# Norm statistics per token: sums of squares as 128x2 numbers, spread by a diagonal product

## The chip, the cores and the metric

The kernel runs on one core of a Trainium2 chip. The metric is device time in microseconds (us) of one execution, the median of several runs. Less is better.

## What is computed

Two layers of a hybrid decoder trunk for 256 tokens of width 2048, float32. Each layer has a mixer (layer 0: dilated attention beside a gated linear recurrence; layer 1: window attention beside a state-space layer) and a ConvFFN, and each of these four parts reads a normed and modulated copy of x. A fifth norm ends the kernel.

```python
def rmsnorm(x, g):
    y = x32 * lax.rsqrt(jnp.mean(x32 * x32, axis=-1, keepdims=True) + NORM_EPS)
    return (y * g.astype(F32)).astype(x.dtype)

def modulate(h, shift, scale):
    return h * (1.0 + scale[:, None]) + shift[:, None]

for layer in range(DEPTH):                      # 2 layers
    h = modulate(rmsnorm(x, norm_mix[layer]), sh1, sc1)
    x = x + g1 * mixer(h)
    h = modulate(rmsnorm(x, norm_ffn[layer]), sh2, sc2)
    x = x + g2 * conv_ffn(h)
return rmsnorm(x, norm_final)
```

shift, scale and gate come from a conditioning vector by the "ada" weights, 1 MB for each column of 128 outputs.

## The kernel before

x lies on the chip transposed: 16 tiles `x[i]`, each with 128 channels on the partitions and the 256 tokens along the free axis. All weights (some 590 MB) are streamed once through six buffers of 1 MB ("w", WB = 6), issued by the SP queue. A weight tile is split by ScalarE (`hi`, L379 or L330) and VectorE (`lo`, L380 or L331) into two float32r parts, and a product is made of three passes (hi by x_hi, hi by x_lo, lo by x_hi). The ada weights go through the same six buffers. Each of their 192 tiles is multiplied with the conditioning and summed by one VectorE instruction of 128x2048 (L221).

A planner (the tile framework) orders each engine's queue before the run, by priorities and by its own estimate of times; an engine works its queue in that order.

`rms` (L258) makes the factor r = 1/sqrt(mean + eps) for all 256 tokens, the same row on all partitions:

- ScalarE squares the 16 tiles (L264).
- In the four later norms VectorE adds the squares (L272), all but the last; then two float32 products with a 128x128 matrix of ones sum over the partitions (each is two passes of 256 columns on TensorE). In the first norm (`on_pe`) TensorE takes all 16 squares, 16 products of two passes.
- ScalarE takes the root of the 128x256 result in PSUM (L280), VectorE its reciprocal, 128x256 (L284).
- In norms two to four `WARM` = (0, 4) puts four more products with ones behind the sum, which only keep TensorE busy (L282).

`modulated_tile` (L287) then makes the tiles that the next weight stage reads: x[i] * A * r on VectorE (L289), + shift on ScalarE (L291, and L293 for the unsplit copy that the first stage uses), the low part on VectorE (L294). The next stage ("slab") goes by k-tiles: seven or fewer PSUM banks take the products of k-tile 0, then of k-tile 1, and so on. So TensorE can't start a slab before k-tile 0 is modulated, and r needs the last piece of x, which needs the last product of the stage before.

PSUM has 8 banks: 3 "mm", 3 "sp", 2 "sx". All matrix products are recorded as L138. The five norms lie at about 11, 408, 1209, 1508 and 2259 us of the profiled span; the last is followed only by the scaling (L996) and the store of the output.

In the first stage (ev_a, up to 84 us) each k-tile needs two ada tiles, which VectorE works at the same time as the small preparations of the state-space layer (L1024 to L1079).

Of the kernel before, what the change touches and what calls it, by code (L numbers as in the profile page):

```python
# [50 lines left out]
WARM = ((0, 0), (0, 4), (0, 4), (0, 4))  # L51
WARM_AT = 13
# [43 lines left out]
def trunk(ctx: ExitStack, tc: tile.TileContext, a: dict, out: bass.AP):  # L96
# [54 lines left out]
    def pin():  # L151
        """the next product comes after all the products before it"""
        pinned[0] = PIN

    def start(chain, prio=0):
        """a chain of work whose parts go between pieces of the weight stream"""
        chains.append((chain, prio))
        advance(chains[-1])
# [15 lines left out]
    # ---------------------------------------------------------------- inputs that are needed first  # L174
# [28 lines left out]
    # silu(c), the same row on all partitions  # L203
# [10 lines left out]
    # ---------------------------------------------------------------- adaLN: one column of 128 at a time  # L214
# [27 lines left out]
    def gate_of(l, q):  # L242
        """gate(i): columns i and i + 1 of a gate"""
# [13 lines left out]
    # ---------------------------------------------------------------- norm  # L257
    def rms(on_pe=False, warm=(0, 0)):  # L258
        """1 / sqrt(mean(x^2) + eps); warm: products that only keep the array's clock up, before the sum and after"""
        ps = pss()  # L260
        acc = None
        for i in range(KT):
# [4 lines left out]
            if on_pe:  # L267
                mm(ps[:, :T], ones, sq, i == 0, i == KT - 1)
            elif acc is None:
                acc = sq  # L270
            elif i < KT - 1:
                V.tensor_tensor(acc, acc, sq, op=ALU.add)  # L272
            if i == WARM_AT:
                for n in range(warm[0]):
                    mm(ps[:, T:], ones, sq, n == 0, n == warm[0] - 1)
        if not on_pe:
            mm(ps[:, :T], ones, acc, True, False)
            mm(ps[:, :T], ones, sq, False, True)
        rt = t1()
        S.activation(rt, ps[:, :T], AF.Sqrt, bias=epsb, scale=1.0 / D)  # L280
        for n in range(warm[1]):
            mm(ps[:, T:], ones, sq, n == 0 and OWN, n == warm[1] - 1)  # L282
        r = t1()
        V.reciprocal(r, rt)  # L284
        return r

    def modulated_tile(i, r, A, sh, full=None):  # L287
        t = t1()
# [9 lines left out]
    def modulator(l, q, g, on_pe=False):  # L298
        """h[i](): the i-th k-tile of the normed and modulated x; q: the chunk of the shift"""
# [21 lines left out]
    # ---------------------------------------------------------------- weight streams  # L321
# [1027 lines left out]
```

## Time and profile before

| | |
|---|---|
| runs | 2271.8, 2273.1, 2273.46 us |
| median | 2273.1 us |
| span of the profiled execution | 2271.8 us |
| TensorE busy | 2209.5 us (97%) |
| VectorE busy | 1812.8 us (80%) |
| ScalarE busy | 1221.4 us (54%) |
| mean granted TensorE clock | 0.988 of full |

In rows of a timeline the first number is the start in us from the span's start, the second the time in us, then engine and line, operation, output <- inputs, shape, and how many instructions the row merges. Matmuls overlap in the array, so of a row with n passes the distance of two starts is (time less one pass's own time) / (n - 1). PEld is TensorE's load of weights, which runs beside its products.

### The profile page before, as it was taken

The page shows a single profiled execution, that of the slowest core. Times are in us where ns is not written, and L with a number is a line of the kernel's source. Part 1 is how long each engine was busy: PE and PEld are TensorE (multiplying, and loading weights), DVE is VectorE, ACT ScalarE, POOL GpSimd, SP SyncE. Part 2 cuts the span into 40 slices and gives each one's busy share as a digit, 9 for nine tenths or more (in the row PEclk, how much of TensorE's full clock was granted, in tenths as well). Part 3 has the DMA queues.
Part 4 walks back from the last instruction along what each step waited for, and adds up shares of the span by engine and source line. Part 5 has one row for each costly group of instructions (what it writes and reads, how often), then busy time and mean ns, then how long its engine had stood idle before and what let it go on. Part 6 is the DMA issues. An engine that isn't in the chain of part 4 may idle for free. (4 is left out here: it accounts for less than half of the span.)

```text
span 2271.8 us, 42923 instructions
## 1 busy us (share of the span) xinstructions
PE 2209.5 (97%) x17498; PEld 2148.6 (95%) x17498; DVE 1812.8 (80%) x2908; ACT 1221.4 (54%) x2056; POOL 4.4 (0%) x12
## 2 busy tenths in 40 slices
PE   7999999998999999999999999999999999999997
PEld 4899989898999999999999899999999999999997
DVE  7789989989998869989778778986888657666655
ACT  3355856444775456654445767644565434544543
POOL 0000000000000000000000000000000000000000
PEclk9999999999999999999999999999999999999998
DMA  9988689888669778888866665967756667655541
GB/s 349 373 337 308 235 303 350 333 327 338 259 242 352 306 295 317 320 336 314 304 238 224 245 254 224 342 222 289 276 181 222 238 244 287 234 185 180 203 181 69
DMA packets 106088, 615.43 MB, mean 271 GB/s; under 512 B 12065, under 2 KB 14625, under 8 KB 54817
## 3 DMA queue, kind: packets, MB, share of 16 engines
q1 hardware_dynamic: 105890, 612.69, 71.9%
q8 instruction: 137, 2.24, 0.4%
q14 instruction: 61, 0.50, 0.1%
HBM read 592.72 MB, written 18.87 MB: 269 GB/s over the span
## 5 line engine op out<-in xcount | busy, mean ns | idle before, releaser
L138 PE MATMUL mm<-t,hi 128*128 128x256 f32 x9568 | 1744.2, 284 | 7.3 <-ACT hi L379 4.3
L138 PEld LDWEIGHTS mm<-t,hi 128*128 128x128 f32 x9568 | 1498.5, 193 | 10.4 <-ACT hi L379 4.7
L138 PE MATMUL mm<-t,lo 128*128 128x256 f32 x4784 | 1356.7, 284 | 5.1 <-DVE lo L331 5.1
L138 PEld LDWEIGHTS mm<-t,lo 128*128 128x128 f32 x4784 | 919.8, 192 | 7.3 <-DVE lo L331 5.8
L330 ACT CAST hi<-w 128x1024 fp32r<-128x1024 f32 (+1 forms) x558 | 565.4, 1016 | 594.4 <-PE mm L138 523.2
L331 DVE TENSOR_TENSOR lo<-w,hi 128x1024 fp32r<-128x1024 f32 (+1 forms) x558 | 657.5, 1182 | 280.2 <-ACT hi L330 276.3
L221 DVE CUSTOM_DVE_ANT_0 ada<-ada,cond 128x2048 f32<-128x2048 f32 x192 | 438.3, 2283 | 22.7 <-DMA ada<-in_adaT 19.7
L379 ACT CAST hi<-w 128x768 fp32r<-128x768 f32 (+2 forms) x160 | 146.4, 921 | 163.1 <-PE sx L138 86.6
L380 DVE TENSOR_TENSOR lo<-w,hi 128x768 fp32r<-128x768 f32 (+2 forms) x160 | 167.4, 1061 | 62.3 <-ACT hi L379 61.6
L138 PE MATMUL sp<-t,hi 128*128 128x256 f32 x832 | 153.6, 283 | 0.0
L138 PEld LDWEIGHTS sp<-t,hi 128*128 128x128 f32 x832 | 130.3, 192 | 0.8 <-ACT hi L379 0.2
L138 PE MATMUL sp<-t,lo 128*128 128x256 f32 x416 | 117.1, 283 | 0.0
L759 DVE SCALAR_TENSOR_TENSOR t<-mm,ffn_p,t 128x255 f32<-128x255 f32 x232 | 110.6, 477 | 4.2 <-ACT t L757 1.7
L138 PEld LDWEIGHTS sp<-t,lo 128*128 128x128 f32 x416 | 79.6, 192 | 0.1
L291 ACT ACTIVATE t<-t,mods 128x256 fp32r<-128x256 f32 x64 | 30.0, 505 | 85.6 <-DVE mods L311 62.8
L138 PE MATMUL sx<-t,t 128*128 128x64 f32 (+2 forms) x480 | 68.3, 283 | 3.3 <-DMA t<-s 1.1
L757 ACT ACTIVATE t<-mm,ffn_p 128x256 f32<-128x256 f32 x116 | 65.0, 560 | 5.6 <-DVE t L759 5.4
L138 PEld LDWEIGHTS sx<-t,t 128*128 128x128 f32 x480 | 61.5, 194 | 5.9 <-issue 3.3
L264 ACT ACTIVATE t<-x 128x256 f32<-128x256 f32 x80 | 31.9, 414 | 59.4 <-DVE x L451 31.9
L138 PE MATMUL mm<-t,w 128*128 128x256 f32 x256 | 56.5, 379 | 0.9 <-ACT t L665 0.9
L138 PEld LDWEIGHTS mm<-t,w 128*128 128x128 f32 x256 | 48.5, 190 | 7.8 <-ACT t L665 1.3
L318 ACT CAST t<-t 128x256 fp32r<-128x256 f32 x102 | 40.2, 402 | 26.1 <-DVE t L763 20.1
(264 smaller groups left out, 1475.1 us busy)
## 6 DMA issues: line engine op xcount, KB each, us to landing
ada<-in_adaT SPq DMA_DIRECT2D x192, 1024.0 KB, 6.5
w<-in_ffn_in SPq DMA_DIRECT2D x116, 1024.0 KB, 6.1
w<-in_ffn_out SPq DMA_DIRECT2D x80, 896.0 KB, 4.7
w<-in_ffn_first SPq DMA_DIRECT2D x48, 896.0 KB, 6.6
w<-in_ev_out SPq DMA_DIRECT2D x16, 1024.0 KB, 6.4
w<-in_ffn_out SPq DMA_DIRECT2D x16, 1024.0 KB, 5.2
w<-in_od_out SPq DMA_DIRECT2D x16, 1024.0 KB, 7.4
w<-in_ev_a SPq DMA_DIRECT2D x16, 896.0 KB, 7.0
```

Of the source, the lines that this page charges most:

```text
L138: keep(PE.matmul(o, l, r, start=start, stop=stop, skip_group_check=True))
L221: V.tensor_tensor_reduce(out=w, in0=w, in1=cond, scale=1.0, scalar=0.0, op0=ALU.mult, op1=ALU.add, accum_out=mods[l][:, j:j + 1])
L264: S.activation(sq, x[i], AF.Square)
L291: S.activation(o[:, 0, :], t, AF.Identity, bias=sh[:, i:i + 1])
L318: S.copy(o[:, 0, :], src)
L330: S.copy(hi[:, :m], w[:, o:o + m])
L331: V.tensor_tensor(lo[:, :m], w[:, o:o + m], hi[:, :m].bitcast(F32), op=ALU.subtract)
L379: S.copy(hi[:, :c], w[:, o:o + c])
L380: V.tensor_tensor(lo[:, :c], w[:, o:o + c], hi[:, :c].bitcast(F32), op=ALU.subtract)
L757: S.activation(c, ps[:, s, :], AF.Identity, bias=fp[:, 3, j:j + 1], scale=fp[:, 2, j:j + 1])
L759: V.scalar_tensor_tensor(c[:, d:], ps[:, s, :T - d], fp[:, 2 - d, j:j + 1], c[:, d:], op0=ALU.mult, op1=ALU.add)
```

## The change

r is made with the tokens on the partitions. `total` makes the square tile the stationary operand and one column of ones the moving one, twice for each tile (128 tokens each), so that the sums of 256 tokens stand as 128x2 numbers in PSUM. The last two squares go to TensorE by themselves, beside the sum of the first 14. Root (ScalarE) and reciprocal (VectorE) work on 128x2. Then VectorE multiplies the identity with each column of r (two 128x128 results, `diag`), one product of ones with diag spreads r over all partitions into another PSUM bank, and ScalarE copies it to SBUF. k-tile 0 reads r from PSUM, the others the copy. The products that only keep TensorE busy are two instead of four and come behind the spread. In the first k-tile of a slab the pass with lo comes before the pass with x_lo.

```diff
-WARM = ((0, 0), (0, 4), (0, 4), (0, 4))
+WARM = ((0, 0), (0, 2), (0, 2), (0, 2))
     def rms(on_pe=False, warm=(0, 0)):
-        ps = pss()
+        ps, row = psx(), pss()
         acc = None
+        def total(v, start, stop):
+            for b in range(2):
+                mm(row[:, b:b + 1], v[:, b * P:(b + 1) * P], ones[:, 0:1], start and b == 0, stop)
         for i in range(KT):
             sq = t1()
             S.activation(sq, x[i], AF.Square)
             if on_pe:
-                mm(ps[:, :T], ones, sq, i == 0, i == KT - 1)
+                total(sq, i == 0, i == KT - 1)
             elif acc is None:
                 acc = sq
-            elif i < KT - 1:
+            elif i < KT - 2:
                 V.tensor_tensor(acc, acc, sq, op=ALU.add)
-        if not on_pe:
-            mm(ps[:, :T], ones, acc, True, False)
-            mm(ps[:, :T], ones, sq, False, True)
-        rt = t1()
-        S.activation(rt, ps[:, :T], AF.Sqrt, bias=epsb, scale=1.0 / D)
+            else:
+                if i == KT - 2:
+                    total(acc, True, False)
+                total(sq, False, i == KT - 1)
+        rt = sm((P, 2))
+        S.activation(rt, row[:, 0:2], AF.Sqrt, bias=epsb, scale=1.0 / D)
+        V.reciprocal(rt, rt)
+        diag = t1((P, 2, P))
+        for b in range(2):
+            V.tensor_scalar_mul(diag[:, b, :], ident, rt[:, b:b + 1])
+        mm(ps[:, :T], ones, diag.rearrange("p b t -> p (b t)"), True, True)
         for n in range(warm[1]):
-            mm(ps[:, T:], ones, sq, n == 0 and OWN, n == warm[1] - 1)
+            mm(row[:, T:], ones, sq, False, n == warm[1] - 1)
         r = t1()
-        V.reciprocal(r, rt)
-        return r
+        S.copy(r, ps[:, :T])
+        return r, ps[:, :T]

     def modulated_tile(i, r, A, sh, full=None):
+        r = r[i == 0]

         # slab(), product():
                 pairs = [(hi, xa[:, 0, bs]), (hi, xa[:, 1, bs]), (lo, xa[:, 0, bs])]
+                if first:
+                    pairs = [pairs[0], pairs[2], pairs[1]]

     # last norm
-    r = rms()
+    r, _ = rms()
```

## Rows read from the trace of the kernel before

**Rows 1.** The page's busy time, share of the span and instructions of TensorE.
```profile
PE 2209.5 (97%) x17498; PEld 2148.6 (95%) x17498; DVE 1812.8 (80%) x2908; ACT 1221.4 (54%) x2056; POOL 4.4 (0%) x12
```

**Rows 2.** Timeline, the second norm, from the last squares to the next stage's first products.
```profile
406.15 0.81 ACT L264 ACTIVATE t<-x 128x256 f32<-128x256 f32 x2 [1.39 <-DVE x L459]
...
407.30 0.41 DVE L272 TENSOR_TENSOR t<-t,t 128x256 f32<-128x256 f32 x1
...
407.77 2.08 PE L138 MATMUL sp<-t,ones 128*128 128x256 f32 x4 [3.81 <-DVE t L272]
...
409.88 0.47 ACT L280 ACTIVATE t<-sp,epsb 128x256 f32<-128x256 f32 x1 [2.92 <-PE sp L138]
...
410.39 1.75 DVE L284 RECIPROCAL t<-t 128x256 f32<-128x256 f32 x1 [0.34 <-ACT t L280]
...
410.41 3.49 PE L138 MATMUL sp<-t,ones 128*128 128x256 f32 x8 [0.56 <-ACT t L280]
...
413.55 0.70 PE L138 MATMUL mm<-t,hi 128*128 128x256 f32 x3
```

**Rows 3.** Timeline, the third norm: the next stage's first products.
```profile
1214.59 1.30 PE L138 MATMUL mm<-t,hi 128*128 128x256 f32 x4
```

**Rows 4.** Timeline, the fourth norm: its sum on TensorE, the next stage's first products.
```profile
1507.61 1.13 PE L138 MATMUL sp<-t,ones 128*128 128x256 f32 x4 [3.60 <-DVE t L272]
...
1512.52 0.72 PE L138 MATMUL mm<-t,hi 128*128 128x256 f32 x3
```

**Rows 5.** Timeline, the last norm: its sum on TensorE.
```profile
2259.58 1.62 PE L138 MATMUL sp<-t,ones 128*128 128x256 f32 x4 [2.21 <-DVE t L272]
```

**Rows 6.** Windows: length; busy us of PE, PEld, DVE, ACT, POOL; PEclk, DMA.
```profile
976.60:980.00 3.40, 3.35 (x30) 3.15 (x29) 3.40 (x6) 1.78 (x5) 0.00 (x0) 1.00 0.45 174
980.10:983.50 3.40, 3.40 (x18) 3.40 (x18) 1.93 (x3) 2.55 (x10) 0.00 (x0) 0.50 0.01 2
...
1208.90:1215.60 6.70, 6.14 (x16) 4.52 (x17) 4.22 (x8) 1.78 (x4) 0.00 (x0) 0.50 0.14 48
1509.20:1512.60 3.40, 3.30 (x9) 2.64 (x9) 3.28 (x5) 1.06 (x4) 0.00 (x0) 0.50 0.84 309
```

**Rows 7.** Timeline, small products of TensorE: before 980, at full, at half clock.
```profile
979.43 0.61 PE L138 MATMUL sx<-t,t 128*128 128x32 f32 x4
...
1264.28 1.10 PE L138 MATMUL sx<-t,t 128*128 128x64 f32 x8 [1.14 <-DMA t<-s]
...
1266.85 1.97 PE L138 MATMUL sx<-t,t 128*128 128x64 f32 x8
```

**Rows 8.** Groups by line and form: busy us, mean ns of one, idle before and releaser.
```profile
L665 ACT COPY t<-sp 128x256 f32<-128x256 f32 x8 | 2.6, 368 | 0.0
...
L569 ACT ACTIVATE sp<-sp 128x8 f32<-128x8 f32 x1 | 0.2, 192 | 0.0
```

**Rows 9.** Groups by line and form, VectorE: the small reciprocal, a 128x128 product.
```profile
L852 DVE RECIPROCAL sm<-sm 128x2 f32<-128x2 f32 x16 | 2.4, 157 | 0.1
...
L1137 DVE TENSOR_TENSOR sm<-pack 128x128 f32<-128x128 f32 x8 | 2.3, 281 | 0.0
```

**Rows 10.** The page's groups: ScalarE's reading of a PSUM bank in the ConvFFN.
```profile
L757 ACT ACTIVATE t<-mm,ffn_p 128x256 f32<-128x256 f32 x116 | 65.0, 560 | 5.6 <-DVE t L759 5.4
```

**Rows 11.** Timeline, the first norm on TensorE and the first slab's start.
```profile
11.02 8.69 PE L138 MATMUL sp<-t,ones 128*128 128x256 f32 x32
...
18.90 2.28 DVE L221 CUSTOM_DVE_ANT_0 ada<-ada,cond 128x2048 f32<-128x2048 f32 x1
...
21.79 1.75 DVE L284 RECIPROCAL t<-t 128x256 f32<-128x256 f32 x1
...
23.64 0.48 DVE L289 SCALAR_TENSOR_TENSOR t<-x,A,t 128x256 f32<-128x256 f32 x1
...
25.13 2.28 DVE L221 CUSTOM_DVE_ANT_0 ada<-ada,cond 128x2048 f32<-128x2048 f32 x1
```

**Rows 12.** A window of the first stage, columns as in rows 6.
```profile
26.00:36.00 10.00, 10.00 (x25) 5.29 (x24) 9.53 (x52) 3.13 (x7) 0.00 (x0) 0.74 0.85 306
```

More of the change, by code (lines that the diff above doesn't have):

```diff
@@ L50 @@
 SPILL_AT = 8
-WARM = ((0, 0), (0, 4), (0, 4), (0, 4))
-WARM_AT = 13
+WARM = ((0, 0), (0, 2), (0, 2), (0, 2))
 OWN = False
@@ L267, in rms @@
             if on_pe:
-                mm(ps[:, :T], ones, sq, i == 0, i == KT - 1)
+                total(sq, i == 0, i == KT - 1)
             elif acc is None:
                 acc = sq
-            elif i < KT - 1:
+            elif i < KT - 2:
                 V.tensor_tensor(acc, acc, sq, op=ALU.add)
-            if i == WARM_AT:
-                for n in range(warm[0]):
-                    mm(ps[:, T:], ones, sq, n == 0, n == warm[0] - 1)
-        if not on_pe:
-            mm(ps[:, :T], ones, acc, True, False)
-            mm(ps[:, :T], ones, sq, False, True)
-        rt = t1()
-        S.activation(rt, ps[:, :T], AF.Sqrt, bias=epsb, scale=1.0 / D)
+            else:
[9 more added lines that the diff above has]
+        mm(ps[:, :T], ones, diag.rearrange("p b t -> p (b t)"), True, True)
         for n in range(warm[1]):
-            mm(ps[:, T:], ones, sq, n == 0 and OWN, n == warm[1] - 1)
+            mm(row[:, T:], ones, sq, False, n == warm[1] - 1)
         r = t1()
-        V.reciprocal(r, rt)
-        return r
+        S.copy(r, ps[:, :T])
+        return r, ps[:, :T]
     def modulated_tile(i, r, A, sh, full=None):
+        r = r[i == 0]
         t = t1()
```

## The prediction

> **What bounds the kernel now.** I read the page's busy shares first: TensorE is busy 2209.5 of 2271.8 us [rows 1], so outside some 62 us of gaps the kernel is TensorE's stream of products, which the change leaves alone. A change to the norms can only move what lies in the gaps. So I read the timeline around each norm next, then windows for the granted clock, then the start.
>
> In the second norm [rows 2] the reader is to see one chain. The last squares end at 406.15 + 0.81 = 406.96. VectorE's last addition starts at 407.30, because a weight split was ahead of it. The two sums (four passes) take from 407.77 to 409.85, the root 0.47, the reciprocal 1.75, and the next stage's first products start at 413.55. TensorE's four extra products (eight passes from 410.41) fill most of the wait and end at about the same time as the first modulated tile. The third norm has the same shape and starts its stage at 1214.59 [rows 3]. In the fourth the sum takes 1.13, as the clock is still full there, and the stage starts at 1512.52 [rows 4]. The last norm's sum takes 1.62 [rows 5].
>
> Two rows on the clock decide much. In the third norm the clock is at half (1.2 of 2.4 GHz) from about 1208.9 to 1215.6, in the fourth from 1509.2 to 1512.6 [rows 6]; in both the half clock reaches past or to the first products of the new stage [rows 3, 4]. A microsecond that the chain gains inside such a stretch lets the slab start earlier but at half speed, so it is worth half. And in the stretch 976.6 to 980.0, TensorE was busy 3.35 of 3.40 us, and the clock still fell to half in the next one [rows 6]. What it ran there, after some full-width passes at its beginning, were 24 passes with only 32 moving columns, the last four of them in a row of the timeline [rows 7]. [...]
>
> **The change, part by part.** I work out each piece against the profiled execution (2271.8 us, the lowest of the three runs; the median is 1.3 above it) and add 1.3 at the end.
>
> *The sum, later norms.* Out: one addition (0.41) with what stood ahead of it on VectorE, and four passes of 256 columns (2.08 at half clock, 1.13 at full). In: for each of three tiles (the sum of 14, and squares 14 and 15) two products of two passes, each with a weight load of 128 columns and one moving column. The trace has no pass of one column. The nearest row is 64 columns: eight passes in 1.10 us at full clock, about 0.12 apart, and in 1.97 at half, about 0.24 apart; 32 columns are no quicker (four in 0.61, 0.11 apart) [rows 7]. So the load sets the distance, and I take the same for one column; the lower bound, which no row excludes, is half of it. The sum of 14 and square 14 are mostly over when square 15 comes, so about six passes and the array's depth remain: 1.0 to 2.0 us after the last square. In the second norm that ends at about 409.0 instead of 409.85: 0.9 gained. I take the same for the third. In the fourth, at full clock, six passes and the depth (1.0) stand against the addition and 1.13: 0.8 to 1.1 with the splits ahead of the addition; I take 1.1. The last norm: 0.6, from 1.62 and the addition against 1.0 to 1.5.
>
> The Trainium skill, "TensorE: Matmul & The Clock Gate", section "LDWEIGHTS (loading the stationary operand)", puts a load at columns / 1.2, 107 ns for 128, with no word of the clock. The full-clock row agrees (about 120 ns); the half-clock row (about 240 ns) doesn't, and I go by the rows.
>
> *The spread, later norms.* Out: root 0.47 and reciprocal 1.75 of 256 columns, 2.22. In: root of 128x2, 0.19 (the nearest is 128x8 [rows 8]); reciprocal 0.16; two products of 128x128, at most 0.28 each, 0.4 to 0.56 together [rows 9]; the spread product of two passes, 0.73 at full clock and 1.16 at half (two of the 0.43 of rows 2 and some 0.3 of depth); the copy, 0.37 [rows 8]; and three more handovers between engines at some 0.05 (as from 407.71 to 407.77). Sum: 2.0 at full clock, 2.5 at half, so minus 0.2 to plus 0.3. The direct reading of PSUM by k-tile 0 would save the copy only if both engines could read the bank together. The ConvFFN has ScalarE waiting for VectorE's reading of the same bank, 5.4 us in all [rows 10], so I charge the copy in full. The Trainium skill, "PSUM — Partial Sum Buffer", section "PSUM bank collisions raise a hardware error", wants two engines kept off one bank at one time; the row agrees.
>
> *Extra products.* Two instead of four, but behind the spread: four passes, 1.72 at half clock, against copy, L289 and L291 (0.37 + 0.48 + 0.51 = 1.4): no gain, at worst 0.3 of delay.
>
> *To the slab.* Second and third norm: 0.9 less 0.3, about 0.6 earlier, inside half clock: 0.3 each. Fourth: 1.1 + 0.2, about 1.3 earlier, half of it inside half clock: 0.7. The last norm has nothing behind it but L996: 0.6 less 0.3 = 0.3 (bounds minus 0.3 and plus 1.0). Together 1.6 us gained; bounds 0 and 6 (all at full clock, with passes at half the distance).
>
> *VectorE.* Per norm 1.75 less 0.7 of reciprocal and one addition are freed. In the later norms VectorE waits there anyway: nothing. The swap of the lo and x_lo passes: no stall on x_lo stands in the waits at a slab's start: nothing; if a lo split were late, up to one split (1.2 us) in a slab.
>
> *The first norm.* Here all 16 tiles go to TensorE: 32 passes of 256 columns [rows 11] become 64 small ones. Before, the 32 took 8.69 us; at full clock a pass is half of the 0.43 that rows 2 show, 0.215, so about seven of them ran at half and the stream itself brought the clock up. [...] At 0.22 each, twice the 0.11 of rows 7, they take 14.1 us, from 11.0 to about 25.4, against 19.7: 5.7 later. Root to copy is 2.5 at half clock, so L289 of k-tile 0 can start at about 28.0 instead of 23.64: 4.4 later. Behind it on TensorE waits the whole first slab. On VectorE, in its queue, wait L289 and, as the order stands, the next ada tile (25.13). VectorE is what this stage runs on, 9.53 of 10 us busy [rows 12], so what it can't fill there is lost. It can fill with an ada tile (2.28) and small preparations, if the planner puts them ahead; and it saves 1.1 of reciprocal. Bounds: minus 1.1 (all filled) to plus 4.4; I take plus 2.5, nearer the upper, since the row before shows the ada tile queued behind L289.
>
> **Sum:** minus 1.6 plus 2.5 = plus 0.9: 2272.7 for the profiled execution, 2274.0 for the median. What this kernel's measurement can tell from no change is 0.2%, 4.5 us, so this is "no change".
>
> **Rivals.**
>
> *Faster: the small passes are cheap and the clock holds.* If one column goes at the load's 0.112 or less at either clock, the first norm's 64 passes end at 18.2 or before, VectorE's 1.1 is gained, and the later norms gain their 0.9 to 1.3 plus 0.2 at full clock. 1.1 + 3 x 1.4 + 1.0 = 6.3: 2266.8. By the page's load alone the first norm's sum would be 64 x 0.107 = 6.8 us (an estimate). For it: the full-clock rows. Against: the half-clock row, and the clock that fell under small passes.
>
> *Slower: the clock comes back later.* Before, the sum's wide passes and eight extra ones ran ahead of each slab. [...] Stretches at half are 3.4 or 6.7 us long in this trace [rows 6]; one that goes on for another 3.4 us costs 1.7. In all of norms two to four that is 5.1: 2274.0 + 5.1 = 2279.1. It decides by whether the clock is back by about two us after the slab's start, as it was. For it: half the wide work. Against: the spread product and the slab follow each other with little gap.
>
> *Slower: VectorE's queue at the start.* The planner may think the small sums quick and put the reciprocal ahead of the first two ada tiles, of which the second ran at 18.90 [rows 11]. VectorE then stands until 25.6, both tiles (4.6) follow, and L289 comes at about 31 instead of 23.64: plus 7.4, less 1.6: 2278.9. Behind one of the two it is plus 5.2: 2276.7, no change.
>
> *The change doesn't do what it says.* The direct reading of PSUM gives nothing, as charged above; it is part of the forecast.
>
> **How the numbers follow.** Forecast, 2269 to 2277.6: 0.55. Faster: 0.20, down to 2266.8. The clock: 0.15, 2277.6 to 2279.1. The queue: 0.10, to 2281 with part of the clock's loss. So faster 0.20, same 0.55, slower 0.25, and 8 in 10 lie from 2267.5 to 2281.
>
> **What would show it.** In the profile after: 64 passes in the first norm, 0.2 apart or more and L289 of tile 0 at about 28 us (right), or 0.11 apart and at 23 or before (wrong, faster). From the last squares' end to the slab's first product, 6.6 us in the second norm before, about 6 after. ScalarE's copy ahead of L289, not beside it. The end of the half-clock stretch against the slab's first product. If the first stage's end doesn't move although the first norm is late, the start had cover that I don't see.

## The result, and the profile after

| | before | after |
|---|---|---|
| median of the runs taken together | 2272.45 us (2271.58 to 2273.46, 4 runs) | 2287.82 us (2284.23 to 2289.19, 4 runs) |
| ratio of after to before | | 1.0064, 95% interval 1.0048 to 1.008 |
| profiled execution, its span | 2271.8 us | 2287.0 us |

The change makes the kernel 15 us slower (11 to 18 by the interval), where 0.9 us more than the 2273.1 of then were forecast, 2274.0, and the range ended at 2281.

The busy line of the page after, which answers to [rows 1]:

```profile
PE 2224.0 (97%) x17560; PEld 2165.4 (95%) x17560; DVE 1807.3 (79%) x2914; ACT 1222.5 (53%) x2061; POOL 4.4 (0%) x12
```

TensorE has 62 more instructions and is busy 14.5 us longer, and the span is 15.2 longer. So its gaps have hardly grown (62.3 us before, 63.0 after); nearly all of the loss stands in its busy time. The largest group of products, of the same number and shape, shows it, before and after:

```profile
L138 PE MATMUL mm<-t,hi 128*128 128x256 f32 x9568 | 1744.2, 284 | 7.3 <-ACT hi L379 4.3
...
L137 PE MATMUL mm<-t,hi 128*128 128x256 f32 x9568 | 1751.8, 285 | 12.8 <-ACT t L300 7.7
```

VectorE is busy 5.5 us less, as meant, and that buys nothing.

Timeline of the profile after, the first norm (start, duration, engine, line, operation, out<-in, count, idle time ahead and its releaser). L283 is now the root, L284 the reciprocal, L287 the diagonal, L292 the copy, L298 the first multiplication of a k-tile; L209 is the tanh of cond (the conditioning vector, made in four quarters), L211 writes a quarter of cond, L220 is an ada tile. It answers to [rows 11]:

```profile
11.08 13.81 PE L137 MATMUL sp<-ones,t 128*128 128x1 f32 x64
...
24.93 0.26 ACT L283 ACTIVATE sm<-sp,epsb 128x2 f32<-128x2 f32 x1 [4.53 <-PE sp L137]
25.21 1.28 ACT L209 ACT_TABLE_LOAD   x1
25.22 0.17 DVE L284 RECIPROCAL sm<-sm 128x2 f32<-128x2 f32 x1 [12.43 <-ACT sm L283]
...
26.50 0.60 ACT L209 ACTIVATE t<-sp 128x512 f32<-128x512 f32 x1
...
27.85 0.63 ACT L211 ACTIVATE cond<-t 128x512 f32<-128x512 f32 x1
...
28.71 2.29 DVE L220 CUSTOM_DVE_ANT_0 ada<-ada,cond 128x2048 f32<-128x2048 f32 x1
...
33.34 2.29 DVE L220 CUSTOM_DVE_ANT_0 ada<-ada,cond 128x2048 f32<-128x2048 f32 x1
...
35.55 0.48 DVE L298 SCALAR_TENSOR_TENSOR t<-x,A,sx 128x256 f32<-128x256 f32 x1
...
37.03 5.42 PE L137 MATMUL mm<-w,t 128*128 128x512 f32 x6 [9.77 <-ACT t L302]
```

The sum is as forecast: 64 passes, 13.81 / 64 = 0.216 us apart, ending at 24.89. What follows isn't. VectorE stands idle for 12.43 us ahead of the small reciprocal, which its queue holds ahead of the ada tiles. But an ada tile, which reads all of cond, couldn't have run in that time either: ScalarE's queue holds the last quarter of cond's tanh (26.50) behind the root, with a table load of 1.28 between them, so that cond is whole only at 28.48. The first ada tile starts at 28.71. Before, it waited for cond too, but that was whole at 16.36:

```profile
16.39 2.29 DVE L221 CUSTOM_DVE_ANT_0 ada<-ada,cond 128x2048 f32<-128x2048 f32 x1 [2.82 <-ACT cond L212]
```

Three ada tiles (28.71, 30.93, 33.34) pass before the first multiplication at 35.55, and the first slab product starts at 37.03. Before, L289 ran at 23.64 [rows 11].

The second norm after, from the last sum products to the first slab product, against [rows 2]:

```profile
412.15 1.05 PE L137 MATMUL sp<-ones,t 128*128 128x1 f32 x8 [1.18 <-ACT t L269]
...
413.24 0.26 ACT L283 ACTIVATE sm<-sp,epsb 128x2 f32<-128x2 f32 x1 [0.83 <-PE sp L137]
413.54 0.17 DVE L284 RECIPROCAL sm<-sm 128x2 f32<-128x2 f32 x1 [0.63 <-ACT sm L283]
413.56 1.38 PE L137 MATMUL sp<-t,ones 128*128 128x256 f32 x4 [0.35 <-ACT sm L283]
413.62 2.27 DVE L220 CUSTOM_DVE_ANT_0 ada<-ada,cond 128x2048 f32<-128x2048 f32 x1
...
415.82 0.48 DVE L287 TENSOR_SCALAR t<-pack,sm 128x128 f32<-128x128 f32 x2
...
416.35 1.22 PE L137 MATMUL sx<-t,ones 128*128 128x256 f32 x2 [1.41 <-DVE t L287]
417.66 0.37 ACT L292 COPY t<-sx 128x256 f32<-128x256 f32 x1 [4.16 <-PE sx L137]
418.07 0.48 DVE L298 SCALAR_TENSOR_TENSOR t<-x,A,sx 128x256 f32<-128x256 f32 x1 [1.71 <-ACT t L292]
...
419.15 0.58 PE L137 MATMUL mm<-t,hi 128*128 128x256 f32 x1 [1.57 <-ACT t L300]
```

Two things stand in the chain that weren't forecast. An ada tile (2.27 us) lies on VectorE between the reciprocal and the diagonal, and the extra products (413.56) run ahead of the spread instead of behind it. They do no harm here, since the ada tile takes longer, but in the third norm they do:

```profile
1222.77 2.08 PE L137 MATMUL sp<-t,ones 128*128 128x256 f32 x4 [0.35 <-ACT sm L283]
1222.95 0.48 DVE L287 TENSOR_SCALAR t<-pack,sm 128x128 f32<-128x128 f32 x2
...
1224.64 1.06 PE L137 MATMUL sx<-t,ones 128*128 128x256 f32 x2
```

The diagonal is ready at 1223.43, and the spread starts at 1224.64, because TensorE is at its extra products.

Windows of the profile after: length; busy us of PE, PEld, DVE, ACT, POOL; granted clock; DMA share; GB/s. They answer to [rows 6]:

```profile
414.30:424.50 10.20, 7.21 (x29) 5.86 (x28) 8.31 (x16) 2.58 (x6) 0.00 (x0) 0.50 0.52 193
888.90:892.20 3.30, 3.30 (x18) 3.30 (x17) 1.16 (x3) 2.35 (x10) 0.00 (x0) 0.50 0.67 253
...
1219.90:1230.00 10.10, 7.58 (x27) 6.42 (x28) 5.05 (x15) 3.66 (x9) 0.00 (x0) 0.50 0.19 61
1523.60:1530.40 6.80, 5.23 (x24) 4.79 (x23) 5.62 (x14) 2.99 (x7) 0.00 (x0) 0.50 0.32 121
```

Each of these stretches is wholly at half clock. By the clock's record they are 10.2, 10.2 and 6.8 us long at the second, third and fourth norm; before they were 6.8, 6.8 and 3.4 there. Two more lie at 889 and 940, between two norms. The work of the one at 889 before:

```profile
879.00:883.00 4.00, 4.00 (x36) 4.00 (x36) 2.66 (x4) 2.58 (x11) 0.00 (x0) 1.00 0.57 182
```

There the clock was full, with 36 passes in 4.00 us against 18 in 3.30.

To see where the 15 us arise I count TensorE's products, leave out those with the ones, and take the start of the n-th in a profile less its start in the profile before. That is the lag of the stream, in us, at places named by their time before:

| kernel | 25 | 285 | 358 | 425 | 529 | 888 | 975 | 1231 | 1519 | 2257 |
|---|---|---|---|---|---|---|---|---|---|---|
| after | 11.9 | 6.9 | 5.4 | 7.9 | 9.5 | 9.9 | 11.4 | 13.3 | 15.1 | 15.1 |
| e1_first_old | 1.0 | -0.3 | -1.5 | 2.6 | 4.4 | 4.7 | 6.2 | 6.9 | 6.4 | 6.4 |
| e2_first_new | 11.7 | 8.3 | 6.7 | 7.3 | 7.3 | 10.4 | 10.4 | 10.4 | 7.6 | 8.0 |
| e6_cond_first | 5.4 | 3.6 | 2.1 | 4.2 | 6.0 | 6.3 | 7.8 | 8.5 | 8.0 | 8.0 |
| e10_diag_act | 1.2 | 1.0 | -0.5 | -1.5 | -0.3 | -1.0 | -1.0 | -0.9 | -1.9 | -1.9 |

After: about 7 us are left of the start at 285, and 5.4 at 358; some 2.5 come at the second norm and 1.6 up to 529; the rest comes in steps of 1 to 2 where the clock is at half for longer. Each row is one profile: in two profiles of one program (e14 below) the lag differs by up to 5.5 us. The last norm (from 2257 on) adds nothing: from the last square's end to the first scaling it takes 3.80 us after and 3.75 before.

The same products, counted by the time in which TensorE is busy with them (us, one profile each):

| kernel | products with the ones | all others (17418 in each) | gaps, as span less busy time |
|---|---|---|---|
| before | 33.9 | 2176.9 | 62.3 |
| after | 39.1 | 2185.5 | 63.0 |
| e1_first_old | 34.8 | 2184.9 | 59.2 |
| e2_first_new | 40.9 | 2175.1 | 65.7 |
| e10_diag_act | 35.4 | 2176.9 | 58.7 |

With the first norm alone changed (e2) the loss is in the longer sum and in gaps. With the later norms alone changed (e1) the gaps are shorter, and the other products, the same ones, take 8.0 us longer: that is the clock, at half for 18 times 3.4 us before the last norm where the profile before has 13, at some 1.7 us each. Part of this is scatter, as two profiles of e14 differ by 3.8 us in this column (2183.2 and 2179.4). On average it is 2183.3 in the four profiles with the changed later norms (after, e1, e6, e12) and 2178.7 in four with the old ones (before, e2, e14 twice), 4.7 apart.

### The profile page after: what moved, and what is told of

Same layout as the page of the kernel before. It is cut to its first block, busy times and chain, and to the rows that moved or that the text cites. A ratio compares the mean times of both kernels' runs of the same rounds, so it can differ in the third digit from the quotient of the medians.

```text
span 2287.0 us, 43061 instructions
## 1 busy us (share of the span) xinstructions
PE 2224.0 (97%) x17560; PEld 2165.4 (95%) x17560; DVE 1807.3 (79%) x2914; ACT 1222.5 (53%) x2061; POOL 4.4 (0%) x12
## 5 line engine op out<-in xcount | busy, mean ns | idle before, releaser
L137 PEld LDWEIGHTS mm<-t,hi 128*128 128x128 f32 x9568 | 1504.3, 193 | 18.3 <-ACT t L300 10.1
L220 DVE CUSTOM_DVE_ANT_0 ada<-ada,cond 128x2048 f32<-128x2048 f32 x192 | 438.6, 2285 | 20.7 <-DMA ada<-in_adaT 20.5
L389 DVE TENSOR_TENSOR lo<-w,hi 128x768 fp32r<-128x768 f32 (+2 forms) x160 | 167.1, 1062 | 60.7 <-ACT hi L388 59.2
```

What stands on the lines that cost most here:

```text
L137: keep(PE.matmul(o, l, r, start=start, stop=stop, skip_group_check=True))
L220: V.tensor_tensor_reduce(out=w, in0=w, in1=cond, scale=1.0, scalar=0.0, op0=ALU.mult, op1=ALU.add, accum_out=mods[l][:, j:j + 1])
L389: V.tensor_tensor(lo[:, :c], w[:, o:o + c], hi[:, :c].bitcast(F32), op=ALU.subtract)
```

## The experiments

Theory A says that there are two separate costs: the first norm (its long sum, and the queues behind it), and the chain of the later norms with the clock. The rivals, with letters of their own, stand in the expectations; a letter is used within its runs. The runs of one group shared a chip and the runs of the kernel before; the medians of that kernel beside them were 2272.7 (e1 to e4), 2272.9 (e5, e6, e8, e9), 2273.5 (e10 to e12), 2273.8 (e13, e14) and 2273.7 us (e15, e14 again). A comparison between groups, as of e12 with e6, e8 with e1 and e3, or e10 with e8, carries the difference of these medians, up to 1.1 us.

### One part at a time

**e1_first_old**: the changed kernel, the first norm as before (later norms changed).

```diff
-            r = rms(on_pe, WARM[g])
+            r = rms_wide() if on_pe else rms(on_pe, WARM[g])   # rms_wide: mm(ps[:, :T], ones, sq, ...) as before
```

> The changed kernel with its first norm as before (16 wide products with ones, root and reciprocal on 128x256); the four later norms as changed. In the traces the stream of products lags the kernel before by 11.9 us at the first slab, by 5.4 us shortly before the second norm, and by 15.1 us at the end. Theory A (both parts cost: the first norm about 5.4 us that last, the later norms about 10): about 2282, 5 to 6 below the changed kernel, 10 above the kernel before. Rival B (the start's lag would be made up anyway, all of the loss is in the later norms): 2287, no gain. Rival C (the later lag is a mere consequence of a stream that is shifted against the clock's stretches and the transfers; the start is the cause of all): 2273.

Measured: 2280.99 us, ratio 1.0043 (1.0029 to 1.0057). It gives back 6.8 us of the 15.

**e2_first_new**: the kernel before, the first norm alone in the new form (there all k-tiles read the copy).

```diff
-            r = rms(on_pe, WARM[g])
+            r = rms_rows() if on_pe else rms(on_pe, WARM[g])   # rms_rows: the changed kernel's sum, root, diagonal, spread, copy
```

> The kernel before with only its first norm changed (64 one-column passes, 128x2 root and reciprocal, spread, copy). Theory A: 5 to 6 us above the kernel before, 2278; its first slab at about 35 us as in the changed kernel, VectorE standing some 12 us ahead of the reciprocal. Rival B: 2272.5. Rival C: 2287.

Measured: 2281.56 us, ratio 1.0033 (1.0021 to 1.0045); 8.8 above before, and more than the 2278 expected. The first slab product is 11.7 us late, as in the changed kernel. The two halves cost 8.8 and 8.3 us alone, 17.1 together, against 15.4 for both: two causes that add, to within the scatter of the runs.

**e4_swap**: the kernel before with the order of the three passes swapped in a slab's first k-tile.

```diff
+                if first:
+                    pairs = [pairs[0], pairs[2], pairs[1]]
```

> The kernel before with only the order of passes changed in a slab's first k-tile (lo before x_lo). Theory A: within 1 us of the kernel before, as TensorE waits for neither there. Rival: it waits for the lo split instead of x_lo: up to 1.2 us in each of some eight slab starts, 2275 to 2282.

Measured: 2275.22 us, ratio 1.0006 (0.9997 to 1.0016): no difference that can be told.

### The first norm

**e6_cond_first**: the changed kernel, the blocks that make cond planned ahead of the norm.

```diff
-        ps = pss()
-        mm(ps, ones[0:1, :], crow[:, c], True, True)
-        ...
+        with urgent(3000):
+            ps = pss()
+            mm(ps, ones[0:1, :], crow[:, c], True, True)
+            ...
```

> The changed kernel, but the four blocks that make cond are planned ahead of the norm, so that on VectorE the first ada tile stands ahead of the reciprocal and only the second and third behind it, and on ScalarE the last tanh of cond stands ahead of the root. Theory A (the first norm's cost is VectorE's queue: the reciprocal ahead of the ada tiles): the first ada tile starts near 17 us as in the kernel before, the first k-tile's multiplication at 30 to 31 us instead of 35.55, the first slab product at about 32 instead of 37.03; of these 5 us some 3 are left at the end, by the share that the start's lag kept in the changed kernel (11.9 at the start, 6.9 at 285 us): about 2284 us. Rival C (the lag of 7 us that is left at 285 us is set by the stream of weights and not by the first product's start): first product at 32 as well, but the lag at 285 us stays at 6.9 and the time at 2288.

Measured: 2284.09 us, ratio 1.0051 (1.0035 to 1.0066), 3.7 below the changed kernel. The first ada tile starts at 12.80, and from the root on the timeline reads:

```profile
23.37 0.26 ACT L284 ACTIVATE sm<-sp,epsb 128x2 f32<-128x2 f32 x1 [4.95 <-PE sp L137]
...
23.83 2.29 DVE L221 CUSTOM_DVE_ANT_0 ada<-ada,cond 128x2048 f32<-128x2048 f32 x1
...
29.16 0.38 DVE L299 SCALAR_TENSOR_TENSOR t<-x,A,sx 128x256 f32<-128x256 f32 x1
...
30.54 5.04 PE L137 MATMUL mm<-w,t 128*128 128x512 f32 x6 [2.74 <-ACT t L303]
```

The 35.55 have become 29.16, and the lag at 285 us is 3.6 instead of 6.9: what is left of the start's lag there goes with the first product's start and isn't set by the weights' stream, as rival C would have it. The sum still takes 13.81 us and ends at 23.33, and the second ada tile (23.83) now lies between reciprocal and diagonal, as it does in the second norm. The edit moves cond on ScalarE and the first ada tile on VectorE together, so the two queues are not told apart by it. The time's interval overlaps that of the changed kernel (1.0048 to 1.008).

**e14_before_cond**: the same edit in the kernel before, as a control.

> The kernel before with the four blocks of cond planned ahead of its norm, and nothing else: a control for the runs that mend the first norm in this way. Theory I (cond's place alone moves the first ada tile and the first slab product forward, whatever the norm): first slab product 1 to 2 us before 25.1, the lead of 2 to 4 us kept to 360 us, 2270 to 2272 us. Theory J (the lead of the mended kernel comes from its shorter sum and chain): first slab product at 25 to 26 us as before, 2272.5 to 2274 us.

Measured: 2270.96 us, ratio 0.9987 (0.9978 to 0.9996), first slab product at 22.56, and the lead was 3.6 us at 360: theory I. Once more beside e15:

> The kernel before with cond planned ahead of its norm, once more beside the other run, so that the two are compared on one chip: 2270 to 2272 us as in its first run.

Measured: 2272.64 us, ratio 0.9994 (0.9985 to 1.0003), and in its profile the first slab product came at 23.76 but the lead was gone at 285. So cond's place is worth 1.0 and 2.9 us in the two medians without the change, of which only one is clear of noise, and as much of e6's 3.7 needn't be a cost of the change. Against this control the new form still costs much in e6: the sums start together (9.52 and 9.55), the new one ends 4.7 us later (23.33 against 18.68), and from there to the first slab product it takes 7.2 us against 3.9.

**e12_cond_bf16**: e6 with the first norm's squares in bfloat16, so that the sum has 32 passes. It rounds the squares, so it is a probe and not a mend that computes the same.

```diff
-            sq = t1()
+            sq = t1(dtype=BF16) if on_pe else t1()
...
-... ones[:, 0:1], start and b == 0, stop)
+... (ones_b if on_pe else ones)[:, 0:1], start and b == 0, stop)
```

> The changed kernel with cond planned ahead of the norm, and in the first norm alone the squares are written as bfloat16 (and summed against bfloat16 ones), so that a product is one pass instead of two and the sum has 32 one-column passes instead of 64. This rounds the squares. Theory (what is left of the first norm's cost when VectorE's queue is mended, 5.4 us at the first slab product, is the length of the sum, whose end came 5.2 us later than before): the sum ends at 20 to 21 us instead of 24.9, the first slab product comes at 26 to 28 us instead of 30.5, and the time is 2 to 4 us below the 2284 of the kernel with cond first alone. Rival (the spread, the diagonal and the ada tile ahead of the first multiplication set it): first slab product at 29.5 or later, the same time within 1 us.

Measured: 2276.38 us, ratio 1.0012 (1.0002 to 1.0022), 7.7 below e6, twice what was expected. The first norm:

```profile
12.48 3.28 PE L137 MATMUL sp<-ones_b,t 128*128 128x1 bf16 x22 [0.61 <-ACT t L272]
...
15.61 1.28 ACT L286 ACT_TABLE_LOAD   x1
...
16.90 0.26 ACT L286 ACTIVATE sm<-sp,epsb 128x2 f32<-128x2 f32 x1
...
24.06 4.54 PE L137 MATMUL mm<-w,t 128*128 128x512 f32 x6 [2.73 <-ACT t L305]
```

The sum ends 7.6 us earlier than in e6 (15.76 against 23.33), and the root starts 6.47 earlier (16.90 against 23.37), as it now waits for a table load on ScalarE instead. The first slab product is 6.48 earlier (24.06 against 30.54). From root to product it is 7.2 us in both. So with cond out of the way a delay of the root passes on to the slab one for one. The sum was shorter than forecast, as the 22 passes follow the squares (0.15 us each) and end with them.

### The later norms

**e3_warm_behind**: the changed kernel with the extra products reading the diagonal, so that they can't run ahead of the spread.

```diff
-            mm(row[:, T:], ones, sq, False, n == warm[1] - 1)
+            mm(row[:, T:], ones, diag.rearrange("p b t -> p (b t)"), False, n == warm[1] - 1)
```

> The changed kernel, but the two products that only keep TensorE busy read the diagonal tile, so that they can't run ahead of the spread product (in the changed kernel the planner put them ahead of it). Theory A: in the third norm the spread then starts at about 0.1 us after the diagonal instead of 1.2 us, in the fourth 0.3 instead of 0.8, in the second no difference (an ada tile on VectorE sets it): 1 to 2 us less, 2286, with the half-clock stretches as long as in the changed kernel. Rival D (the hole of 1.5 us between the spread and the slab is why the clock comes back late; the extra products now fill it): half-clock stretches shorter by 3.4 us in up to three norms, 1.7 us each: 2281 to 2284.

Measured: 2281.56 us, ratio 1.0039 (1.0025 to 1.0052), 6.3 below the changed kernel. That is more than the order alone explains: in the third norm the sum's end to the first multiplication falls from 3.72 to 2.73 us, in the second nothing changes (4.86, the ada tile). Besides, by the clock's record of its one profile the stretch at half in the third norm is 6.8 us instead of 10.2, worth 1.7, as rival D has it, and the time lies where D put it.

**e8_late_behind**: e1 and e3 together.

> The changed kernel with both single edits at once: the first norm as before, and in the later norms the two extra products read the diagonal tile, so that they run behind the spread. Theory A (two causes that lie in different stages and add): the first norm gave back 6.8 us and the order of the extra products 6.2, so 2287.8 - 13.0 = 2274.8 us, 2 us above the kernel before, with half-clock stretches of about 10.2, 6.8 and 6.8 us at the second, third and fourth norm against 6.8, 6.8 and 3.4 before. Rival D (what the second edit gave was luck of where the half-clock stretches fall, and does not add): 2279 to 2281.

Measured: 2277.79 us, ratio 1.002 (1.001 to 1.0029). It lies between the two: 3.2 below e1, with intervals that touch. So the 6.3 of e3 did not repeat, and about 3 is the order's worth in this place. The third norm:

```profile
1216.32 1.22 PE L137 MATMUL sx<-t,ones 128*128 128x256 f32 x2 [1.07 <-DVE t L287]
...
1217.34 1.91 PE L137 MATMUL sp<-t,ones 128*128 128x256 f32 x4
...
1219.06 0.58 PE L137 MATMUL mm<-t,hi 128*128 128x256 f32 x1
```

The extra products now lie between the spread and the slab, and end just as it is ready.

**e9_late_behind4**: e8 with four extra products.

```diff
-WARM = ((0, 0), (0, 2), (0, 2), (0, 2))
+WARM = ((0, 0), (0, 4), (0, 4), (0, 4))
```

> The same kernel (first norm as before, extra products behind the spread) with four extra products after each sum as the kernel before has, instead of two. Theory B (the fewer full-width products are what brings the full clock back later): the half-clock stretches go back to 6.8, 6.8 and 3.4 us and the time is 1.7 to 3.4 us below the one with two products, 2271 to 2273. Rival E (TensorE's queue: two more products of 0.43 to 0.87 us lie between the spread and the first slab product, or end before it anyway): the same within 1 us, or 1 us above.

Measured: 2282.55 us, ratio 1.0037 (1.0024 to 1.0049), 4.8 above e8. Neither theory gave as much. Theory B falls here: in e9's profile the stretches at half are no shorter than in e8's (10.2, 6.8 and 3.4 us in both, and one of 3.4 more ahead of the fourth norm in e9). E was right in kind. In the third norm:

```profile
1214.64 3.09 PE L137 MATMUL sp<-t,ones 128*128 128x256 f32 x8
...
1215.30 0.48 DVE L310 SCALAR_TENSOR_TENSOR t<-x,A,sx 128x256 f32<-128x256 f32 x1 [1.72 <-ACT t L292]
...
1217.38 0.47 PE L137 MATMUL mm<-t,hi 128*128 128x256 f32 x1
```

The eight passes last until 1217.7, while the first tile was multiplied at 1215.30; from multiplication to slab it is 2.08 us instead of 1.07 (2.36 and 2.02 in the second and fourth norm, about 1.07 in e8). That is 1.0 to 1.3 in each of three norms, some 3.2; the rest of the 4.8 isn't accounted for.

**e5_warm2**: the kernel before with two extra products for four, and nothing else.

> The kernel before with two instead of four extra products behind each sum, and nothing else. Theory B (the fewer full-width products bring the full clock back later): half-clock stretches 3.4 us longer in one to three norms, so 1.7 to 5 us above the kernel before, 2274.5 to 2278. Rival E (the products bridge too little of the wait for it to matter): 2272.7 as before, or up to 1 us less.

Measured: 2276.32 us, ratio 1.002 (1.0008 to 1.0031), 3.4 above before. The windows at the three norms:

```profile
405.50:415.60 10.10, 8.61 (x29) 6.82 (x30) 9.56 (x17) 2.69 (x6) 0.00 (x0) 0.50 0.64 231
1211.00:1221.10 10.10, 8.47 (x28) 6.67 (x29) 6.82 (x14) 3.10 (x8) 0.00 (x0) 0.50 0.12 40
1508.00:1518.10 10.10, 8.23 (x27) 6.43 (x28) 7.39 (x17) 3.09 (x7) 0.00 (x0) 0.50 0.50 192
```

Three stretches of 10.1 us at half clock where before had 6.8, 6.8 and 3.4, though the sum is the old wide one and the chain the old one. The time agrees with theory B, and so does this profile. How firm the stretches are is another matter: with four extra products the same program (e14) had 6.8, 6.8 and 10.2 us in one profile and 6.8, 6.8 and none in the other. So the 3.4 us in the median are shown, and that they come by these three stretches is likely but not shown.

**e10_diag_act**: e8 with the diagonal made on ScalarE.

```diff
-            V.tensor_scalar_mul(diag[:, b, :], ident, rt[:, b:b + 1])
+            S.activation(diag[:, b, :], ident, AF.Copy, scale=rt[:, b:b + 1])
```

> The kernel with the first norm as before and the extra products behind the spread, with the diagonal tile made on ScalarE (two activations that scale the identity) instead of VectorE. Theory F (in the second norm the diagonal waits 2.27 us behind an ada tile that VectorE runs between the reciprocal and it): from the sum's end to the first k-tile's multiplication 4.87 us become about 2.8 in the second norm and stay at 2.7 to 2.9 in the third and fourth; the second norm's lag shrinks by 2 us, the time by 1.5 to 2.5 us from 2277.8. Rival G (the ada tile's column is needed by the first multiplications anyway, so that it runs ahead of them wherever the diagonal is made): no change in the 4.87 us and the same time.

Measured: 2273.94 us, ratio 1.0007 (0.9997 to 1.0018), 3.9 below e8. The second norm and its windows:

```profile
408.42 2.27 DVE L220 CUSTOM_DVE_ANT_0 ada<-ada,cond 128x2048 f32<-128x2048 f32 x1
408.54 0.69 ACT L287 ACTIVATE t<-pack,sm 128x128 f32<-128x128 f32 x2 [0.23 <-DVE sm L284]
...
410.95 0.48 DVE L310 SCALAR_TENSOR_TENSOR t<-x,A,sx 128x256 f32<-128x256 f32 x1 [0.25 <-ACT t L292]
```

```profile
405.60:412.20 6.60, 4.78 (x15) 3.81 (x16) 4.90 (x10) 2.86 (x9) 0.00 (x0) 0.50 0.87 302
412.60:416.00 3.40, 3.40 (x31) 3.40 (x30) 2.62 (x8) 1.78 (x4) 0.00 (x0) 1.00 0.62 242
```

The ada tile (408.42) still follows the reciprocal, but the diagonal is made beside it. From the sum's end to the first multiplication the 4.87 us are 2.95: theory F. The half-clock stretch is over by 412.6; in e8 it was 10.2 us long. That difference, worth 1.7, would explain why the gain is above the 2 us of the chain.

**e11_no_copy**: e10 without the copy, all k-tiles multiplied by the spread in PSUM.

```diff
-        r = t1()
-        S.copy(r, ps[:, :T])
-        return r, ps[:, :T]
+        return ps[:, :T], ps[:, :T]
```

> The same kernel (diagonal on ScalarE, first norm as before, extra products behind the spread) without the copy out of PSUM: all sixteen k-tiles are multiplied by the spread in PSUM. Theory H (the copy stands whole on the path, because ScalarE's copy and VectorE's read of the one bank take turns): the first multiplication 0.4 us earlier in each of the four later norms, 1.2 to 1.6 us below the kernel with the copy, and each multiplication 0.04 us longer (0.48 for 0.44), hidden. Rival (the bank held through sixteen multiplications delays the next user of its buffer, or VectorE becomes the pace): the same time or 1 to 3 us above.

Measured: 2276.05 us, ratio 1.001 (1.0001 to 1.002). From the sum's end to the first multiplication it is 2.61, 2.53 and 2.54 us where e10 has 2.95, 2.94 and 2.68. So the copy stood on the path, but its 0.1 to 0.4 us a norm don't come out in the time, which is if anything above e10's; the intervals overlap, and why isn't settled.

### All mended

**e13_both_mended**: the changed kernel with the edits of e3, e6, e10 and e12.

> The changed kernel with all four mends at once: cond planned ahead of the norm and the first norm's squares in bfloat16 (one pass for two), the extra products behind the spread, the diagonal made on ScalarE. Theory (the change's cost is these four places and nothing else): the start lies 1 to 4 us ahead of the kernel before up to 360 us, as with the first two mends alone, the later norms cost 0 to 1.5 us less than before, as with the last two alone, and the time is 2270 to 2272 us. Rival (what is won early is lost where a stretch of half clock falls otherwise, 1.7 us for each 3.4 us of it): 2274 to 2276.

Measured: 2272.67 us, ratio 0.9994 (0.9986 to 1.0003). The 15 us are gone, and nothing is won, though part of the mend is e12's bfloat16 sum, which rounds, and part may be cond's place, which the kernel before can have too. The control with cond ahead and the old norms has 2271.0 and 2272.6.

**e15_cond_late**: e10 with cond planned ahead; against e14 it differs in the later norms alone.

> The kernel before with cond planned ahead of its first norm (which alone gave 2271.0 us) and the later four norms in the changed form with both mends (extra products behind the spread, diagonal on ScalarE; with the first norm as before and cond in its old place this gave 2273.9). If the later norms in the mended form are worth nothing either way, 2270.5 to 2271.5 us and no difference from the 2271.0; if their shorter chain counts once the start no longer differs (second norm 1.5 us, fourth 2.3 us from the last square to the first slab product), 2268 to 2270.

Measured: 2272.92 us, ratio 1.0 (0.9992 to 1.0008), and e14 beside it 2272.64: no difference between them. In its profile the chains of norms two to four, from the last square to the first slab product, are 4.82, 5.54 and 4.15 us, 3.8 shorter in sum than in the profile before, and the median doesn't show it. The lowest of all was the kernel before with cond ahead; its interval lay below 1 in the first set of runs (0.9978 to 0.9996) and took in 1 in the second, so a version that surely beats before wasn't found.

## Why the prediction was wrong

Two of its terms failed: what follows the first norm's sum (plus 2.5 forecast, 8.8 measured alone in e2) and the later norms (minus 1.6 forecast, plus 8.3 alone in e1). The sums and the small operations in them were sized rightly.

**The bound** was read wrongly. The prediction has it that the change leaves TensorE's stream alone and can only move what lies in some 62 us of gaps. The gaps grew by 0.7 us. The products with the ones took 5.2 us more, and the 17418 others, which the change leaves alone in number, 8.6 more in these two profiles (4.7 on the average of several), at a clock that was at half for longer.

**The first norm's sum** was right: 25.4 forecast as its end, 24.89 measured, from 0.22 us a pass, twice the 0.11 of [rows 7]; the 64 passes went at 0.216.

**What follows the first sum** is the step that failed most. It was put at "about 28.0" for L289 and at plus 2.5 us, from bounds of minus 1.1 and plus 4.4. L298 came at 35.55 and the part alone costs 8.8 us (e2). The 2.5 rested on the planner putting an ada tile ahead of the reciprocal. It did the contrary, and the rival on VectorE's queue, given a chance of 0.10, had that order: reciprocal ahead of both ada tiles, L289 at about 31. It was 4.5 us short, since ScalarE's queue was left out: cond's last tanh stands behind the root, with its table load, so the first ada tile can't start when VectorE is free at 25.98 but at 28.71. And a third ada tile (33.34) goes ahead of L298. The upper bound of the term, 4.4, lay below the price of a rival in the same text, 7.4. With cond out of the way (e6) the start is still 5.4 us later than before: 3.6 by the sum's end (23.33 against 19.71) and 1.8 by what lies between that and the slab (7.2 against 5.4).

**Cover at the start** was about right as a share. Of 4.4 us the prediction kept 2.5; of the 11.9 us lag of the first slab product 6.9 were left at 285 us, and in e2 8.3 of 11.7, with 8.0 at the end. What was wrong was the delay that the share was taken of.

**The later norms** were put at 1.6 us gained; alone they cost 8.3 (e1). The chain's own length is not what cost this. From the last square's end to the first slab product it takes 6.74, 6.32 and 4.28 us after, where before took 6.58, 5.97 and 5.72. So the fourth norm gained its 1.4 as forecast (1.3); the second and third lost 0.2 and 0.4 in place of gaining 0.6. Sums and small operations were sized rightly: in the second norm the sum ends 0.8 us after the last square (2.88 before), the root takes 0.26, the reciprocal 0.17, the diagonal 0.48, the spread 1.22, the copy 0.37. What ate the gain in the second and third are two matters of order: the ada tile ahead of the diagonal (2.27; e10) and the extra products ahead of the spread (1.2 us in the third norm; e3, e8). The prediction had written "Two instead of four, but behind the spread"; in the program they stood behind it, but on TensorE ahead, since they only read a square that had long been there. That these two orders are the cause the runs show: with the one mended the 8.3 are 4.9 (e8), with both 0.4 (e10). How they cost more than the chain's length is seen in the clock, below. In e1's profile the clock accounts for the whole loss; by the averages it is some 4 to 5 us, and how the 8.3 divide stays open. The last norm, forecast 0.3 faster, was the same.

**The copy** was charged in full, and rightly. L298 waits 1.71 us in the row at 418.07 with the copy as its releaser; VectorE's first multiplication never runs beside ScalarE's copy, and without the copy (e11) it comes 0.1 to 0.4 us earlier. The row that the prediction read this from [rows 10] names a releaser and no bank; e11 is what bears it out. The Trainium skill, "PSUM — Partial Sum Buffer", section "PSUM bank collisions raise a hardware error", wants two engines kept off one bank at one time; the trace agrees, as no row has the two beside each other.

**The clock coming back later**, a rival with 0.15, happened in kind. By its own point of decision, the clock back by about two us after the slab's start, it was 5.4, 2.9 and 4.9 us behind that start in norms two to four (in the second: slab at 419.15, clock back at 424.5), where before it was 0.0, 1.0 and 0.1. In the profile after, the stretch is 3.4 us longer in each of the three, 1.7 each, the 5.1 that the rival named. Other profiles put the size lower: with the changed form of these norms (after, e1, e6, e12) the stretches there add to 27, 24, 20 and 27 us, with the form before (before, e2, e14 twice) and with e4's to 17, 20, 24, 14 and 10. On average that is some 7.7 us more at half, worth 3.8. Of the rival's "half the wide work" e5 tests the extra products alone (3.4 us slower).

**The range** failed in the way the cases were combined. Queue and clock were priced as alternatives, each with a chance of its own, each with the other terms kept at their forecast. They are in different stages and nothing excludes one by the other: 2278.9 and 5.1 more give 2284.0, above the 2281 at which the range ended. With the 4.5 us that the queue's price lacked it would be 2288.5, but that this is near the 2287.8 measured is luck: such a sum has 11.9 us for the start, where e2 shows 8.8, and 3.5 for the later norms, where e1 shows 8.3.

**What stays open.** In single profiles part of the lag is chance. Stretches at half clock that no norm touches come and go between executions. The kernel of e14 has one at 877 and one at 928 us in its first profile and neither in its second (on another chip); windows of the first and, below, of the second at the same work:

```profile
877.20:880.40 3.20, 3.20 (x17) 3.20 (x16) 0.70 (x3) 2.44 (x9) 0.00 (x0) 0.50 0.61 245
928.40:931.60 3.20, 3.20 (x18) 3.20 (x17) 0.99 (x3) 2.27 (x10) 0.00 (x0) 0.50 0.03 13
```

```profile
879.00:883.00 4.00, 4.00 (x35) 4.00 (x36) 3.90 (x6) 2.20 (x8) 0.00 (x0) 1.00 0.82 258
930.00:934.00 4.00, 4.00 (x36) 4.00 (x36) 3.26 (x5) 2.16 (x10) 0.00 (x0) 1.00 0.25 96
```

In both profiles 24 passes with 32 moving columns run here (873.6 to 876.3 in the first, 878.9 to 881.6 in the second), as in the stretch of the kernel before at whose end the prediction saw the clock fall [rows 6, 7]; in the first the clock falls behind them, in the second it stays full. So one such row does not tell what the next execution does. And up to 2 x 1.7 us of the changed kernel's lag, the stretches at 889 and 940, can't be put down to the change from its one profile. What ties a longer wait to a longer stretch at half is not shown beyond the profiles above. The 6.3 us of e3 against the 3.2 of e8, the 4.8 of e9 against 3.2 worked out, and e11 against e10 are of the size of that scatter and weren't settled.

## What to carry to other kernels

A shorter chain must be read in the order that each engine's queue will have: name for every new operation what the planner can put between it and the next, and what stands behind its wait, on every engine and not on the longest alone. Work that is only there to fill a wait has to depend on something that comes after the work it must not delay. Mechanisms that lie in different stages add: price them together before the range is closed. And the clock's stretches in a single profile are one draw: read them in several before a cost is put down to them.

## What the runs showed of the hardware

**One-column passes.** Two-pass float32 products with one moving column and a weight load each were 0.216 us apart for all 64 passes of the first sum, and eight took 1.05, 1.87 and 1.19 us in the later norms; the wide passes that they replace sped up under way (32 in 8.69 us [rows 11]). The first six 128x512 passes of the slab then took 5.42 us, 0.90 each, and three of them later (45.73) 1.45, 0.48 each. So the engine was busy without a break from 11.08 to 24.89, and was still at half pace in its next products. The windows of this stretch show a granted clock of 1.00, but the first record of the clock in this profile lies at 42.3; here the pace has to be read from the passes. The Trainium skill, "TensorE: Matmul & The Clock Gate", section "LDWEIGHTS (loading the stationary operand)", puts a load of 128 columns at 107 ns, by which 64 passes would take 6.8 us, an estimate; the trace has twice that.

**Half clock that comes and goes.** The stretches at half are 3.4, 6.8, 10.2 or, once, 13.7 us long in these profiles, and whether one follows the same products differs between two executions of the same program: the two profiles of e14, on two chips, have 18 and 14 times 3.4 us of them before the last norm. At 1.7 us each that is 6.8 us, so a difference of a few us between single profiles of this kernel can be that alone.
